# A hybrid conv and gated-DeltaNet block: first products of three projections tile by tile, and a last norm in halves

## Chip, cores and metric

One core of one Trainium2 chip. The metric is device time in microseconds of one execution of the whole block; lower is better.

## The reference

The block is two half-step SwiGLU feed-forward layers around a mixer, with norms in fp32, for 1024 tokens of 1024 channels:

```python
h = h + 0.5 * swiglu_ffn(rmsnorm(h, ffn1_norm), ffn1_w_in, ffn1_w_out)
u = rmsnorm(h, mix_norm) @ w_mix_in
...
h = h + jnp.concatenate([y_conv, y_gdn], axis=-1) @ w_mix_out
h = h + 0.5 * swiglu_ffn(rmsnorm(h, ffn2_norm), ffn2_w_in, ffn2_w_out)
return rmsnorm(h, final_norm)
```

The hidden width of the feed-forward layers is 2816. The mixer is a short gated convolution beside a chunked gated delta rule of four heads.

## The kernel before

**Products.** Activations lie with channels on the 128 partitions and half of the tokens (512) along the row: `h[hf][d]`, token half `hf`, channel tile `d` of eight. Every large product is one level of Strassen's method in Winograd's form: seven products of half size from blocks of the activations (A11, A12, S1, nS2, S3, S4, A22) and of the weights (B11 to B22, T1 to T4, the T being differences of B). Each fp32 factor is split in two parts, high and low: `split` casts on ScalarE (L102) and subtracts on VectorE (L103). `mm3` multiplies high by high, low by high, high by low (L191 to L193), three matmuls of 128x128 by 512 tokens that add into one PSUM bank. T sums are made on POOL (`pool_tt`, L110) in a ring of four buffers; weights arrive by SP's DMA queue in a ring of eight raw tiles; their parts, whi and wlo, are in a ring of seven.

**Order of the work.** `task(run, prep, load)` appends to a list; `run_tasks` goes through it, calling a task's prep 4 and its load 9 places ahead of its run. `mm3` calls `tick`, and `later(n, f)` calls f after n more of these; a norm uses it: `after(n, m)` calls `reduce` (sums of squares, L225) after n and `spread` (factors to all partitions, L243) m later. Each engine has its own queue in the order that results.

**First two pairs.** `all_pairs` runs the seven products for pairs of output tiles; it is called three times, for the first FFN's input (about 50 to 100 us), for the mixer's (700 to 760) and for the second FFN's (1295 to 1350). Each starts while the second half's norm is still to come. Once the factors `rb` are there, `Blocks.sums(0)` makes S1 and nS2 from the second half (L300, L301, four tiles each) and splits them; `sums(1)` makes A22, S3 and S4; `sums(2)` splits A22 and S4. `Pair.body` yields p6 (T2 x nS2), p5 (T1 x S1), p7 (T3 x S3), p4 (T4 x A22) and p3 (B22 x S4), each of 12 matmuls and each with its T made just ahead. p7 ends in the sum c on VectorE (L389, L390) into which the bank is read.

**The output products.** `ffn_out` runs seven products of 11 steps of 12 matmuls into two sets of four banks. The last two, S3 x T3 and A22 x T4, end in `add`: VectorE adds half of each bank into the residual (L554), and ScalarE and VectorE make the sum of squares for the next norm. `t1_done` and `out_t1` start the norm of the first half after the fifth product. At the end of the program `scale_out` scales the residual by the last norm's factors and weight on VectorE (L1387) and POOL (L1385) and stores it in eight DMAs of 256 KB per half (L1389).

Of the kernel before, what the change touches and what calls it, by code (L numbers as in the profile page):

```python
# [12 lines left out]
P = 128  # L13
D = 1024
# [42 lines left out]
def tile_hybrid(  # L57
# [209 lines left out]
    class Blocks:  # L267
# [53 lines left out]
    class Pair:  # L321
# [41 lines left out]

        def body(self):
# [44 lines left out]
    def all_pairs(pairs, x, norm2, between={}):  # L409


        norm2.then(lambda: x.sums(0, norm2.rb))
        for a in (0, 2):
            for n, two in enumerate(zip(*(p.body() for p in pairs[a:a + 2]))):
                if a == 0 and n in (1, 2):
                    task(None, lambda n=n: norm2.then(lambda: x.sums(n, norm2.rb)))
                for t in two:
                    task(*t)
# [77 lines left out]
    def ffn_out(acc, fill, g_dr, w_out, t1_done, t2_done):  # L496
# [8 lines left out]
        def step(banks, a, b, k, start):  # L505
# [27 lines left out]
            def run():  # L533
                x, w = ops["x"], ops["w"]
                if start and k == 0:
                    banks[:] = [psum() for _ in range(KH)]
                for d in range(KH):
                    ds = slice(d * P, (d + 1) * P)
                    mm3(banks[d], w[0][:, ds], w[1][:, ds], x[0], x[1], start and k == 0, k == NK - 1)

            task(run, ready, loads)

        def product(banks, a, b, start, *to, then=None, after=None):
            for k in range(NK):
                step(banks, a, b, k, start)
# [4 lines left out]
            def add():  # L550
                for d in range(KH):
# [9 lines left out]
            task(add)  # L561
# [8 lines left out]
        product(ba, "A22", "T4", True, "C21", then=t2_done)  # L570
# [19 lines left out]
    with ExitStack() as stack:  # L590
# [74 lines left out]
        def t1_done():  # L665
# [3 lines left out]
            nm[0].after(26, 4)  # L669
# [703 lines left out]
    with ExitStack() as stack:  # L1373
# [4 lines left out]
        def scale_out(hf):  # L1378
            rb = temp(F32, "rbs")
            nc.scalar.copy(out=rb, in_=last[hf].rb)  # L1380
            for d in range(KT):
                a = acc[hf][d]
                if d % 3 == 1:
                    nc.scalar.activation(out=a, in_=a, func=AF.Copy, scale=vcol(V_N["final"] + d))
                    nc.gpsimd.tensor_tensor(out=a, in0=a, in1=rb, op=ALU.mult)  # L1385
                else:
                    nc.vector.scalar_tensor_tensor(out=a, in0=a, scalar=vcol(V_N["final"] + d), in1=last[hf].rb,  # L1387
                                                   op0=ALU.mult, op1=ALU.mult)
                (nc.scalar if hf and d % 2 else nc.sync).dma_start(out=out[hf, d], in_=a)  # L1389
# [7 lines left out]
        ffn_out(acc, fill, g_dr, w2_out, out_t1, lambda d: last[1].square(d, nc.vector))  # L1397
        run_tasks()
        last[1].reduce()
        last[1].spread()  # L1400
        scale_out(1)
# [67 lines left out]
```

## Time and profile before

| | |
|---|---|
| median of 3 runs | 1960.46 us (1956.25 to 1960.53) |
| profiled execution | 1959.77 us, span 1958.0 us |
| busy: TensorE | 1833.8 us, 94% |
| VectorE, ScalarE, POOL | 68%, 38%, 37% |
| mean granted clock of TensorE | 0.971 |
| DMA | 312.45 MB, 160 GB/s over the span |

Busy time counts a matmul until its modelled end, so a TensorE that is busy all the time is not by that at its peak. The granted clock is 1.00 at the higher of its two levels and 0.50 at the lower.

### The profile page before, as it was taken

The numbers are of one execution on the slowest core, as the hardware profiler recorded it, in microseconds if no ns is written. First come the engines' busy times: TensorE is split into PE (matmuls) and PEld (weight loads), VectorE is DVE, ScalarE is ACT, GpSimd is POOL, SyncE is SP. The second block draws the span as 40 slices with busy tenths as digits, with TensorE's granted clock in tenths as the row PEclk, the third lists the DMA queues.
The fourth block names the chain that finished last, engine by engine and source line by source line (L and its number), as shares of the span: only waits on it lengthen the run. The fifth ranks groups of instructions, "written<-read, shape, count | busy, mean of one in ns | idle before, by whom it ended". The sixth has DMA issues, their size and how long they took to land.

```text
span 1958.0 us, 25016 instructions
## 1 busy us (share of the span) xinstructions
PE 1833.8 (94%) x8512; PEld 1493.6 (76%) x8512; DVE 1338.5 (68%) x1991; ACT 750.0 (38%) x1517; POOL 733.3 (37%) x510
## 2 busy tenths in 40 slices
PE   5799999999999899987799989998999999999996
PEld 4578888888888777676678877776888888888884
DVE  4876666567865797776974356688666566677655
ACT  6422323223544453377332243452323222344433
POOL 1464455355331434145311001036454355435142
PEclk9899999999999999998999979998999999999998
DMA  7144343437883423477742176423343434487532
GB/s 281 33 161 128 118 140 127 140 108 257 311 270 113 140 97 102 141 245 252 222 135 80 61 263 183 164 92 102 127 139 127 140 109 160 150 292 274 193 108 97
DMA packets 194512, 312.45 MB, mean 160 GB/s; under 512 B 27856, under 2 KB 48336, under 8 KB 194384
## 3 DMA queue, kind: packets, MB, share of 16 engines
q1 hardware_dynamic: 191216, 305.28, 47.0%
q10 hardware_dynamic: 3168, 5.57, 0.9%
q8 instruction: 67, 1.10, 0.2%
q14 instruction: 61, 0.50, 0.1%
HBM read 228.44 MB, written 82.33 MB: 159 GB/s over the span
## 4 chain that ended last, share of the span: by engine, by line
PE 74%; DVE 13%; issue 4%; DMA 3%; POOL 3%; ACT 3%; SPq 0%; POOLq 0%; DVEq 0%; ACTq 0%
PE ps_ps L192 20%; PE ps_ps L191 20%; PE ps_ps L193 20%; PE ps_mm L191 3%; PE ps_mm L192 3%; PE ps_mm L193 3%; DVE wlo L103 3%; PE ps_aux L862 1%; DVE lo L103 1%; DVE xb L1034 1%; DVE sv L1030 1%; DVE cv L774 1%; POOL T L110 1%; DMA raw<-w_in 1%; DVE h L301 1%
## 5 line engine op out<-in xcount | busy, mean ns | idle before, releaser
L191 PE MATMUL ps_ps<-hi,whi 128*128 128x512 f32 x1400 | 554.1, 396 | 23.0 <-DVE c L389 11.4
L193 PE MATMUL ps_ps<-hi,wlo 128*128 128x512 f32 x1400 | 552.7, 395 | 13.0 <-DVE wlo L103 12.9
L192 PE MATMUL ps_ps<-lo,whi 128*128 128x512 f32 x1400 | 553.0, 395 | 5.3 <-DVE lo L103 5.2
L103 DVE TENSOR_TENSOR wlo<-raw,whi 128x512 fp32r<-128x512 f32 x280 | 267.3, 964 | 119.4 <-ACT whi L102 118.4
L103 DVE TENSOR_TENSOR wlo<-T,whi 128x512 fp32r<-128x512 f32 x244 | 235.3, 978 | 144.5 <-ACT whi L102 142.4
L191 PEld LDWEIGHTS ps_ps<-hi,whi 128*128 128x128 f32 x1400 | 266.8, 191 | 85.4 <-issue 12.3
L193 PEld LDWEIGHTS ps_ps<-hi,wlo 128*128 128x128 f32 x1400 | 267.3, 191 | 71.7 <-DVE wlo L103 16.0
L192 PEld LDWEIGHTS ps_ps<-lo,whi 128*128 128x128 f32 x1400 | 266.9, 191 | 63.1 <-DVE lo L103 8.0
L110 POOL TENSOR_TENSOR T<-raw 128x512 f32<-128x512 f32 x144 | 224.6, 1561 | 232.3 <-DMA raw<-w_out 91.5
L191 PE MATMUL ps_ps<-ghi,whi 128*128 128x512 f32 x616 | 241.8, 393 | 7.2 <-ACT whi L102 7.2
L192 PE MATMUL ps_ps<-glo,whi 128*128 128x512 f32 x616 | 241.9, 393 | 1.4 <-DVE glo L103 1.4
L193 PE MATMUL ps_ps<-ghi,wlo 128*128 128x512 f32 x616 | 241.7, 393 | 1.2 <-DVE wlo L103 1.2
L102 ACT CAST whi<-raw 128x512 fp32r<-128x512 f32 x280 | 170.2, 617 | 86.1 <-PE ps_mm L192 19.1
L102 ACT CAST whi<-T 128x512 fp32r<-128x512 f32 x244 | 146.4, 617 | 81.4 <-POOL T L110 44.8
L191 PE MATMUL ps_mm<-hi,whi 128*128 128x512 f32 x384 | 158.0, 412 | 0.9 <-DVE u L400 0.9
L192 PE MATMUL ps_mm<-lo,whi 128*128 128x512 f32 x384 | 155.2, 404 | 1.2 <-DVE lo L103 1.2
L193 PE MATMUL ps_mm<-hi,wlo 128*128 128x512 f32 x384 | 154.2, 402 | 1.4 <-DVE wlo L103 1.4
L103 DVE TENSOR_TENSOR glo<-raw,ghi 128x512 fp32r<-128x512 f32 x154 | 128.9, 838 | 38.8 <-ACT ghi L102 37.2
L191 PEld LDWEIGHTS ps_ps<-ghi,whi 128*128 128x128 f32 x616 | 116.3, 189 | 33.6 <-ACT whi L102 8.4
L193 PEld LDWEIGHTS ps_ps<-ghi,wlo 128*128 128x128 f32 x616 | 116.3, 189 | 28.0 <-DVE wlo L103 2.7
L192 PEld LDWEIGHTS ps_ps<-glo,whi 128*128 128x128 f32 x616 | 116.4, 189 | 27.3 <-DVE glo L103 2.1
L110 POOL TENSOR_TENSOR T<-raw,T 128x512 f32<-128x512 f32 x50 | 73.3, 1465 | 167.2 <-DMA raw<-w_in 129.3
(226 smaller groups left out, 2286.5 us busy)
## 6 DMA issues: line engine op xcount, KB each, us to landing
raw<-w_in SPq DMA_DIRECT2D x264, 256.0 KB, 4.6
raw<-w_out SPq DMA_DIRECT2D x154, 256.0 KB, 4.3
raw<-w_qkv SPq DMA_DIRECT2D x36, 256.0 KB, 3.4
f1S<-S SPq DMA_DIRECT2D x33, 256.0 KB, 5.0
raw<-f1A SPq DMA_DIRECT2D x33, 256.0 KB, 3.9
raw<-f1S SPq DMA_DIRECT2D x33, 256.0 KB, 3.7
f2S<-S SPq DMA_DIRECT2D x33, 256.0 KB, 5.0
raw<-f2A SPq DMA_DIRECT2D x33, 256.0 KB, 4.5
```

The source lines that it names most:

```text
L102: tc.keep_in_program_order(nc.scalar.copy(out=hi, in_=src))
L103: nc.vector.tensor_tensor(out=lo, in0=src, in1=hi.bitcast(F32), op=ALU.subtract)
L110: tc.keep_in_program_order(nc.gpsimd.tensor_tensor(out=out, in0=in0, in1=in1, op=op))
L191: nc.tensor.matmul(out=ps, lhsT=whi, rhs=xhi, start=start, stop=False, skip_group_check=True)
L192: nc.tensor.matmul(out=ps, lhsT=whi, rhs=xlo, start=False, stop=False, skip_group_check=True)
L193: nc.tensor.matmul(out=ps, lhsT=wlo, rhs=xhi, start=False, stop=stop, skip_group_check=True)
L301: nc.vector.tensor_tensor(out=s2, in0=s2, in1=s1, op=ALU.subtract)
L774: nc.vector.scalar_tensor_tensor(out=acc, in0=u[:, i:i + HALF], scalar=vcol(wc + i), in1=acc, op0=ALU.mult, op1=ALU.add)
L862: nc.tensor.matmul(out=ps[:, sl], lhsT=lhs[:, sl], rhs=rhs[:, sl], start=start, stop=stop)
L1030: nc.vector.tensor_tensor(out=tv, in0=lrow[:, lo:hi].unsqueeze(2).broadcast_to([nb, n, j + 1]), in1=xrow[:, 0:j + 1].unsqueeze(1).broadcas ...
L1034: nc.vector.tensor_tensor(out=xv, in0=xv, in1=tv, op=ALU.subtract)
```

## The change

Four places change. (1) In `all_pairs` the products T1 x S1 and T2 x nS2 of the first two pairs run tile by tile: for each k, both products of both pairs, in four banks; S1's split follows directly on its scaling. The preps of T1 and T2 come first for both pairs, and A22's and S4's splits come behind T3's prep. (2) Two norms are started earlier: `after(26, 4)` and `after(30, 4)` become `after(14, 4)`. (3) In the second FFN's last product the last four steps are held and run bank by bank, each bank's `add` right behind it. (4) The last norm and its scaling run in two halves of 256 tokens, with 16 stores of 128 KB, ten on SP's queue and six on ScalarE's; the final weight is applied ahead for three of eight channel tiles (`gain`).

```diff
                     nc.vector.tensor_tensor(out=s2, in0=s2, in1=s1, op=ALU.subtract)
+                    b["S1"][k] = split(s1, slot)
                     b["nS2"][k] = split(s2, slot)
-                for k in range(KH):
-                    b["S1"][k] = split(h[1][k], slot)
...
+        def both(self, k):
+            if k == 0:
+                self.z, self.y = psum(), psum()
+            ks = slice(k * P, (k + 1) * P)
+            for ps, t, s in ((self.z, "T1", "S1"), (self.y, "T2", "nS2")):
+                w = self.w[t]
+                mm3(ps, w[0][:, ks], w[1][:, ks], *self.x.b[s][k], k == 0, k == KH - 1)
+            if k == KH - 1:
...
+                nc.vector.tensor_tensor(out=self.u2[:, 3:HALF + 3], in0=self.y, in1=self.p1[:, 3:HALF + 3], op=ALU.add)
...
+            products = list(zip(*(p.body() for p in pairs[a:a + 2])))
+            if a == 0:
+                for one, two in zip(*products[:2]):
+                    task(None, one[1], one[2])
+                    task(None, two[1])
+                for k in range(KH):
+                    task(lambda k=k: [p.both(k) for p in pairs[:2]])
+            for n, two in enumerate(products):
+                if a == 0 and n == 1:
+                    task(None, lambda: norm2.then(lambda: x.sums(1, norm2.rb)))
+                if a > 0 or n > 1:
+                    for t in two:
+                        task(*t)
+                if a == 0 and n == 2:
+                    task(None, lambda: norm2.then(lambda: x.sums(2, norm2.rb)))
...
-        product(ba, "A22", "T4", True, "C21", then=t2_done)
+        product(ba, "A22", "T4", True, "C21", then=t2_done, by_tile=by_tile)
...
+            for d in range(KH):
+                task(lambda d=d: [one(d, i == KH - 1) for i, one in enumerate(held)] and add([d]))
...
-            nm[0].after(26, 4)
+            nm[0].after(14, 4)
...
-            last[0].after(30, 4)
-            last[0].then(lambda: scale_out(0))
+            last[0].after(14, 4)
+            last[0].then(lambda: [gain(0, d) for d in range(KT) if pre_scaled(d)] and scale_out(0))
...
+        ffn_out(acc, fill, g_dr, w2_out, out_t1, out_t2, by_tile=True)
         run_tasks()
-        last[1].reduce()
-        last[1].spread()
-        scale_out(1)
...
+        for i in range(2):
+            for b in range(2 * i, 2 * i + 2):
+                nc.tensor.matmul(out=last[1].rb[:, b * P:(b + 1) * P], lhsT=rs[:, b:b + 1].broadcast_to([P, P]),
+                                 rhs=ident, start=True, stop=True)
+            scale_out(1, slice(2 * i * P, (2 * i + 2) * P))
```

How the order moves, in three places. First VectorE's queue in the first FFN's first products, before. Here h_81 to h_84 are S1's tiles, h_73 to h_76 those of nS2 and then of S3, h_85 to h_88 those of A22; T1_522 and T1_544 (before) are the two pairs' T1.

```order
L103 TENSOR_TENSOR lo_610<-h_74,hi_609 128x512
L313 TENSOR_TENSOR h_76<-h_76,h_88 128x512
L103 TENSOR_TENSOR lo_618<-h_75,hi_617 128x512
L103 TENSOR_TENSOR wlo_646<-T1_522,whi_645 128x512
L103 TENSOR_TENSOR lo_626<-h_76,hi_625 128x512
L103 TENSOR_TENSOR wlo_666<-T1_544,whi_665 128x512
L380 TENSOR_TENSOR u2_682<-ps_ps_669,p1_439 128x512
L103 TENSOR_TENSOR lo_685<-h_85,hi_684 128x512
L380 TENSOR_TENSOR u2_729<-ps_ps_716,p1_441 128x512
```

The same place in the changed kernel, where T1_593 and T2_595 belong to the second pair:

```order
L103 TENSOR_TENSOR lo_586<-h_84,hi_585 128x512
L307 SCALAR_TENSOR_TENSOR h_85<-h_85,vs_66,ps_ps_548 128x512
L103 TENSOR_TENSOR lo_590<-h_76,hi_589 128x512
L103 TENSOR_TENSOR wlo_598<-T2_595,whi_597 128x512
L103 TENSOR_TENSOR wlo_616<-T1_593,whi_615 128x512
L312 TENSOR_TENSOR h_73<-h_73,h_85 128x512
L307 SCALAR_TENSOR_TENSOR h_86<-h_86,vs_66,ps_ps_548 128x512
L307 SCALAR_TENSOR_TENSOR h_87<-h_87,vs_66,ps_ps_548 128x512
```

T1's last low part stood behind three of S3's subtractions; now it stands ahead of all of S3's, right behind S1's and nS2's. A little further on the same queue, before, where s4 is S4:

```order
L103 TENSOR_TENSOR lo_689<-h_86,hi_688 128x512
L103 TENSOR_TENSOR lo_693<-h_87,hi_692 128x512
L103 TENSOR_TENSOR lo_697<-h_88,hi_696 128x512
L103 TENSOR_TENSOR lo_701<-s4_598,hi_700 128x512
L103 TENSOR_TENSOR lo_705<-s4_606,hi_704 128x512
L103 TENSOR_TENSOR lo_709<-s4_614,hi_708 128x512
L103 TENSOR_TENSOR lo_713<-s4_622,hi_712 128x512
L103 TENSOR_TENSOR wlo_734<-T3_731,whi_733 128x512
L103 TENSOR_TENSOR wlo_746<-T3_743,whi_745 128x512
```

And in the changed kernel:

```order
L103 TENSOR_TENSOR lo_666<-h_76,hi_665 128x512
L103 TENSOR_TENSOR wlo_688<-T3_685,whi_687 128x512
L103 TENSOR_TENSOR wlo_706<-T3_703,whi_705 128x512
L103 TENSOR_TENSOR lo_728<-h_85,hi_727 128x512
L374 TENSOR_TENSOR u2_773<-ps_ps_678,p1_441 128x512
L103 TENSOR_TENSOR lo_732<-h_86,hi_731 128x512
L103 TENSOR_TENSOR lo_736<-h_87,hi_735 128x512
L103 TENSOR_TENSOR lo_740<-h_88,hi_739 128x512
```

T3's low parts stood behind the eight subtractions for A22 and S4; now they stand ahead of them. On TensorE's queue the twelve matmuls of T2 x nS2, which took nS2's tiles one after the other for one pair, and those of T1 x S1 behind them, are now mixed: three matmuls with a tile of S1 into one bank, three with the tile of nS2 into another, then the same for the second pair. Third, TensorE's queue at the end of the program, before:

```order
L193 MATMUL ps_ps<-ghi,wlo 128x512
L225 MATMUL ps_ps<-cs,nacc 128x1 [waits DVE_49]
L225 MATMUL ps_ps<-cs,nacc 128x1 x3
L243 MATMUL ps_ps<-cs,rs 128x128 [waits Pool_49]
L243 MATMUL ps_ps<-cs,rs 128x128 x3
```

and now, where L1453 is the reduction and L1460 the spread:

```order
L193 MATMUL ps_ps<-ghi,wlo 128x512
L1453 MATMUL ps_ps<-cs,nacc 128x1 [waits DVE_49]
L1453 MATMUL ps_ps<-cs,nacc 128x1
L1453 MATMUL ps_ps<-cs,nacc 128x1 [waits DVE_49]
L1453 MATMUL ps_ps<-cs,nacc 128x1
L1460 MATMUL ps_ps<-cs,last_rs 128x128 [waits Pool_49]
L1460 MATMUL ps_ps<-cs,last_rs 128x128
L1460 MATMUL ps_ps<-cs,last_rs 128x128 [waits DVE_49,Pool_49]
L1460 MATMUL ps_ps<-cs,last_rs 128x128
```

The reduction and the spread are in two parts, and the second part of each has a wait of its own for VectorE. In the same way the norm's spread at the end of the first FFN stands 36 matmuls earlier on TensorE's queue, and that at the end of the second FFN 48 earlier.

## Rows read from the trace of the kernel before

**Rows 1.** The page: the chain that ended last, shares of the span by engine.

```profile
PE 74%; DVE 13%; issue 4%; DMA 3%; POOL 3%; ACT 3%; SPq 0%; POOLq 0%; DVEq 0%; ACTq 0%
```

**Rows 2.** Windows, 100 to 640 us: each engine's busy us (x instructions), granted clock, DMA share, GB/s.

```profile
100.00:640.00 540.00, 538.38 (x2367) 443.79 (x2366) 364.82 (x430) 181.74 (x324) 244.57 (x161) 1.00 0.50 169
```

**Rows 3.** Waits of PE, 50 to 100 us: for what, us in total, times, longest.

```profile
PE ps_ps L193 <- DVE wlo L103: 7.3, 2, 6.2
PE ps_ps L191 <- DVE c L389: 2.9, 1, 2.9
```

**Rows 4.** Timeline of DVE at 57.9 us: start, length, line, operation, out<-in.

```profile
57.92 1.77 DVE L301 TENSOR_TENSOR h<-h 128x512 f32<-128x512 f32 x1
```

**Rows 5.** Timeline of POOL at 71 us; in brackets its idle time before and what ended it.

```profile
71.34 2.20 POOL L110 TENSOR_TENSOR T<-raw 128x512 f32<-128x512 f32 x1 [9.90 <-DVE wlo L103]
```

**Rows 6.** Windows: five stretches right after waits of PE, with their matmuls and granted clock.

```profile
71.25:75.25 4.00, 4.00 (x10) 3.21 (x11) 4.00 (x6) 3.13 (x6) 3.89 (x2) 0.51 0.14 34
88.80:92.00 3.20, 3.20 (x9) 2.53 (x8) 2.32 (x4) 0.00 (x0) 1.07 (x1) 0.50 0.02 5
733.75:737.25 3.50, 3.50 (x9) 2.73 (x10) 1.68 (x2) 1.05 (x2) 3.40 (x3) 0.53 0.15 44
1328.98:1334.98 6.00, 6.00 (x15) 4.70 (x16) 4.05 (x4) 2.28 (x4) 5.82 (x4) 0.52 0.29 90
1918.30:1921.80 3.50, 3.46 (x8) 2.57 (x9) 3.50 (x5) 3.50 (x7) 1.70 (x2) 0.51 0.47 137
```

**Rows 7.** Waits of PE, 700 to 760 us (mixer's projection).

```profile
PE ps_ps L193 <- DVE wlo L103: 3.0, 2, 2.2
PE ps_ps L191 <- DVE c L389: 2.5, 1, 2.5
PE ps_ps L191 <- ACT whi L102: 1.1, 1, 1.1
```

**Rows 8.** Waits of PE, 1295 to 1350 us (second FFN's first products).

```profile
PE ps_ps L191 <- DVE c L389: 3.2, 1, 3.2
PE ps_ps L193 <- DVE wlo L103: 2.6, 2, 2.2
PE ps_ps L191 <- ACT whi L102: 1.2, 1, 1.2
```

**Rows 9.** Waits of PE, 640 to 680 us (end of the first FFN).

```profile
PE ps_ps L191 <- ACT whi L102: 3.1, 2, 2.2
PE ps_ps L193 <- DVE wlo L103: 1.2, 2, 0.8
PE ps_ps L192 <- DVE glo L103: 0.7, 1, 0.7
```

**Rows 10.** Windows: VectorE's load at 60, 632 and 660 us.

```profile
60.00:70.00 10.00, 4.65 (x18) 3.23 (x18) 10.00 (x17) 6.19 (x12) 1.45 (x1) 0.92 0.00 0
632.00:642.00 10.00, 10.00 (x54) 8.54 (x53) 0.76 (x3) 0.00 (x0) 3.84 (x4) 1.00 0.21 56
660.00:670.00 10.00, 7.83 (x34) 5.81 (x32) 6.93 (x8) 5.28 (x10) 9.65 (x7) 1.00 0.46 157
```

**Rows 11.** Waits of PE, 1880 us to the end.

```profile
PE ps_ps L191 <- ACT whi L102: 4.1, 1, 4.1
PE ps_ps L225 <- DVE nacc L211: 3.5, 1, 3.5
```

**Rows 12.** Timeline of all engines, 1942 us to the end.

```profile
1942.83 1.87 PE L225 MATMUL ps_ps<-cs,nacc 128*128 128x1 f32 x8 [3.49 <-DVE nacc L211]
...
1948.78 3.38 DVE L1387 SCALAR_TENSOR_TENSOR h<-h,vs,ps_ps 128x512 f32<-128x512 f32 x5 [3.88 <-ACT rbs L1380]
...
1950.12 3.98 ACTq L1389 DMA_DIRECT2D out_dram<-h  x4
```

**Rows 13.** DMA issues: out<-in, queue, issues, KB each, median us from issue to landing.

```profile
raw<-w_out SPq DMA_DIRECT2D x154, 256.0 KB, 4.3
...
y_dr<-zt SPq DMA_DIRECT2D x16, 128.0 KB, 2.2
```

More of the change, by code (lines that the diff above doesn't have):

```diff
@@ L493, in early_heads, with ffn_out @@
             task(*p.head2())
[L496 removed]
+    def ffn_out(acc, fill, g_dr, w_out, t1_done, t2_done, by_tile=False):
         tsum = {}
@@ L503, in get, with step @@
             return load(w_out[2 * k + row][:, c * HALF:(c + 1) * HALF])
-        def step(banks, a, b, k, start):
+        def step(banks, a, b, k, start, held=None):
             r, ops = {}, {}
@@ L537, in run, with one, product @@
                 for d in range(KH):
[L538 to L543, printed above, removed]
+                    one(d, k == NK - 1)
+            def one(d, stop):
+                x, w = ops["x"], ops["w"]
+                ds = slice(d * P, (d + 1) * P)
+                mm3(banks[d], w[0][:, ds], w[1][:, ds], x[0], x[1], start and k == 0, stop)
+            if held is None:
+                task(run, ready, loads)
+            else:
+                held.append(one)
+                task(None, ready, loads)
+        def product(banks, a, b, start, *to, then=None, after=None, by_tile=False):
+            held = []
             for k in range(NK):
-                step(banks, a, b, k, start)
+                step(banks, a, b, k, start, held if by_tile and k >= NK - KH else None)
                 if KH <= k < KT:
@@ L548, in product, with add @@
                         task(lambda tile_=tile_: fill(*tile_))
-            def add():
-                for d in range(KH):
+            def add(ds=range(KH)):
+                for d in ds:
                     for n in to:
@@ L559, in add @@
                     after()
-            task(add)
+            if not by_tile:
+                task(add)
+                return
+            for d in range(KH):
+                task(lambda d=d: [one(d, i == KH - 1) for i, one in enumerate(held)] and add([d]))
         ba, bb = [], []
@@ L1393, in out_t1, with out_t2 @@
                 last[0].square(d)
-            last[0].after(30, 4)
-            last[0].then(lambda: scale_out(0))
-        ffn_out(acc, fill, g_dr, w2_out, out_t1, lambda d: last[1].square(d, nc.vector))
-        run_tasks()
-        last[1].reduce()
-        last[1].spread()
-        scale_out(1)
+            last[0].after(14, 4)
+            last[0].then(lambda: [gain(0, d) for d in range(KT) if pre_scaled(d)] and scale_out(0))
+        def out_t2(d):
+            last[1].square(d, nc.vector)
+            if pre_scaled(d):
+                gain(1, d)
+        ffn_out(acc, fill, g_dr, w2_out, out_t1, out_t2, by_tile=True)
+        run_tasks()
+        last[1].rb = psum()
+        sums = psum()
+        ms, rs = (const.tile([P, 4], F32, name=n) for n in ("last_ms", "last_rs"))
+        for i in range(2):
+            two = slice(2 * i, 2 * i + 2)
+            for b in range(2 * i, 2 * i + 2):
+                nc.tensor.matmul(out=sums[:, b:b + 1], lhsT=last[1].acc[:, b * P:(b + 1) * P], rhs=ones[:, 0:1],
+                                 start=True, stop=True)
+            nc.vector.tensor_scalar(out=ms[:, two], in0=sums[:, two], scalar1=1.0 / D, scalar2=EPS,
+                                    op0=ALU.mult, op1=ALU.add)
+            nc.gpsimd.tensor_tensor(out=rs[:, two], in0=ms[:, two], in1=pneg[:, two], op=ALU.pow)
+        for i in range(2):
+            for b in range(2 * i, 2 * i + 2):
+                nc.tensor.matmul(out=last[1].rb[:, b * P:(b + 1) * P], lhsT=rs[:, b:b + 1].broadcast_to([P, P]),
+                                 rhs=ident, start=True, stop=True)
+            scale_out(1, slice(2 * i * P, (2 * i + 2) * P))
         while queue:
```

30 lines of the change are left out of this document (15 added, 15 removed).

## The prediction

> **What bounds the kernel now.** I read the chain of waits first: TensorE holds 74% of the chain that ended last and VectorE 13% [rows 1], so time is to be had only where TensorE stands still. The windows by stage come next. In the longest undisturbed stretch TensorE is busy 538.38 of 540 us with 2367 matmuls at a granted clock of 1.00 [rows 2], which is 0.2275 us per matmul; whatever an earlier stage saves therefore passes through to the end. Then I read the waits of TensorE in the five stretches that the change touches, the stretches behind those waits in which the clock is at the lower of its two levels [rows 6], and the timeline of the last 20 us. A matmul at the lower level takes 4.0/10 = 0.40 us in the first of those stretches, so a stretch costs its length less 0.2275 us for each matmul in it.
>
> The sum is made against the profiled execution, 1959.77 us (span 1958.0); the median of the runs shown, 1960.46, is 0.7 above it. A measurement of this kernel can tell about 0.3% (5.9 us) from no change.
>
> **Part 1: first two pairs of the three input projections (first FFN, mixer, second FFN).** Nothing is computed less. Moved: VectorE's subtractions (lo parts), POOL's T3 and T4, ScalarE's casts, and the matmuls of T1·S1 and T2·nS2, which now run k by k.
>
> First FFN. TensorE waits 7.3 us for wlo parts (6.2 for T1's, 1.1 for T3's) and 2.9 for the c sum [rows 3]; two slow stretches follow, 4.0 - 10 x 0.2275 = 1.7 and 3.2 - 9 x 0.2275 = 1.2 [rows 6]. What is late is T1's low part: its subtraction stands behind those of nS2, S1 and three of S3. T3 needs a buffer that this subtraction reads last, and POOL sat 9.90 us until it had, T3 starting at 71.34 [rows 5]. In the new order T1's last subtraction stands eleven places earlier on VectorE (69 to 58), and T3's two stand before those of A22 and S4. So 7.3 + 2.9 + 2.9 = 13.1 us can go. What comes: a tile k of both pairs is 12 matmuls, 2.7 us, and VectorE must deliver four operations for it, 4 x 0.68 = 2.7 us by the duration of one (3.38/5 [rows 12]), but up to 1.77 each where POOL works beside it [rows 4]; I allow 1.7 us of small waits. T3's cast and subtraction still come behind the S3 parts: 3.0 us. T4: 0.7. A slow stretch after T3's wait: 2.0, between the two seen. Gain 13.1 - 7.4 = **5.7**, bounds 1 (only the c wait and little else goes) and 11.
>
> Mixer. Goes: 3.0 + 2.5 + 1.1 = 6.6 of waits [rows 7] and 1.5 of slow clock (3.5 - 9 x 0.2275) [rows 6] with 1.2 for the stretch after the c wait, taken from the like one in the first FFN. Comes: a weight of the second head, whose subtraction now stands three lo parts later, 1.0, and 0.7 at T4. Gain 9.3 - 1.7 = **7.6**, bounds 3 and 9.3.
>
> Second FFN. Goes: 3.2 + 2.6 + 1.2 = 7.0 [rows 8], slow clock 6.0 - 15 x 0.2275 = 2.6 [rows 6] and 1.2 as before, 10.8. Comes: the second head's weight stands behind 15 VectorE operations in place of 12 here, and POOL's T and s4 sums run beside them. Three at 0.68 are 2.0 us, at 1.77 they are 5.3; I take 2.5, since TensorE wanted it only just before it was ready. A slow stretch behind that wait 2.0, T4 0.5. Gain 10.8 - 5.0 = **5.8**, bounds 1 and 10.
>
> **Part 2: norm of the first half, end of the first FFN** (call count 26 to 14: 12 triples of matmuls, 36 x 0.2275 = 8.2 us sooner). The eight scalings and eight subtractions behind that norm now land where VectorE is busy 0.76 of 10 us [rows 10], in front of the casts of the last product. They cost about the 16 x 0.68 = 11 us that they took before, covered by that idle time. TensorE's waits behind it, 3.1 for whi, 1.2 for wlo and 0.7 for glo [rows 9], should go: 5.0, of which I leave 0.5. **4.5**, bounds 2 and 5.5. The sum of squares is done before the earlier call, so the reduce waits for nothing; if POOL's adds were late, TensorE's queue would hold there for a few POOL operations.
>
> **Part 3: norm at the end of the second FFN and the last product** (30 to 14: 48 matmuls, 10.9 us sooner). POOL's scaling of the first half came between the T4 sums before; TensorE waited 4.1 us for whi [rows 11] and then ran a slow stretch, 3.5 - 8 x 0.2275 = 1.7 [rows 6]. With the norm ahead of the final product's preparations the casts are done in time. Gain 5.8 - 0.3 = **5.5**, bounds 3 and 6.5. The 44 triples run bank by bank only in their last four steps; all of those casts must be there before the first of four banks ends, and VectorE's queue should reach the last of them about 2 us before it is wanted (an estimate, from some 14 operations of 0.68 us behind the adds).
>
> **Part 4: the end.** Now all four banks' adds come behind the last matmul; TensorE waits 3.5 us for the sum of squares [rows 11]. In the new order only bank 3's add, square and sum remain, three operations of about 0.68, so 3.5 - 2.0 = 1.5 is saved. Behind it stand the reduction at 1942.83, VectorE's five scalings from 1948.78 (3.38 us), and the output's issues, the last from 1950.12 on; the span ends at 1958.0 [rows 12]. Two halves overlap the scaling of one with the output of the other. The final bytes are 1 MB in place of 2 MB; the first half leaves about 2 us sooner. TensorE's second reduction waits for VectorE's reading of the first bank, and the second spread for VectorE's reading of the first half's, so the halves are only partly abreast. Added are a second copy of the factors, five more operations on VectorE and three on POOL, each of half the length, and eight more output issues; they lie beside each other or beside the first half's output. I take 2.5 here: **4.0** in all, bounds 1 and 5.5. Sixteen output transfers of 128 KB take the place of eight of 256 KB; the only 128 KB stores in the trace land in 2.2 us against 4.3 for a load of 256 KB [rows 13], so I charge nothing for the size.
>
> A rule speaks against this. The Trainium skill, page "DMA: Bandwidth & Descriptors", section "Rules for kernel authors", wants 1 MiB or more in one transfer for the highest bandwidth, by which pieces of 128 KB would be the wrong way. By that rule part 4 would gain only the 1.5 of the adds; the rows on 128 KB do not agree, and it is rival (d).
>
> Sum: 5.7 + 7.6 + 5.8 + 4.5 + 5.5 + 4.0 = 33.1. From 1959.8: **1927 us**.
>
> **Rivals.** (a) *The waits move.* VectorE is full in this stretch (10.00 of 10 us in 60 to 70 us [rows 10]) and the change takes no operation off it; so the three sites stay as long as they are and only parts 2 to 4 pay, 14.0: 1946 us. For it: the full engine. Against: the waits are on single late operations, and those are moved ahead. 13%.
> (b) *Slower: the tile order keeps TensorE below its clock.* Working tile by tile over four banks TensorE stops for each lo part; should the clock go to its lower level through those 48 matmuls at each site, each costs 0.40 - 0.2275 = 0.17 more, 8.3 us a site, 25 in three; with the waits of part 1 as they are, and parts 2 to 4 gained, 1959.8 - 14.0 + 25 = 1971 us. It decides from the granted clock at 57 to 70 us, 724 and 1300. For it: 10 matmuls at 0.51 right behind a wait of 6.2. Against: 660 to 670 us lost 2.2 of 10 us in waits and stayed at 1.00 [rows 10]. 3%. The Trainium skill, page "TensorE: Matmul & The Clock Gate", section "A second HAM failure mode: psum-queue depth-cycling", describes this: a kernel that cycled through banks and paused between groups swung between the two clock levels. By that rule 1971 would come; the trace, cycling four banks at 1.00 for 540 us, does not agree.
> (c) *The held steps of the last product come late.* Four steps' casts must all be there at one time, and a load of raw data takes 4.3 us to land [rows 13]. If the first bank's fourth step waits for one, 4.3 us of part 3 are lost: 1931 us. 8%.
> (d) *The output in small pieces is no quicker,* each issue paying its fixed time twice as often: the 2.5 of part 4 is lost, 1930 us. 4%.
> (e) *Nearly every moved wait vanishes,* with all bounds at their upper ends: 11 + 9.3 + 10 + 5.5 + 6.5 + 5.5 = 47.8, 1912 us. For it: the waits have few causes. 8%.
> (f) *No measurable change,* because a gain in one product is waited for in the next: 4%. Something unforeseen and slower: 2%.
>
> **How the numbers follow.** My forecast has 58%. Faster by over 0.3%: 58 + 13 + 8 + 4 + 8 = 91 of 100; within 0.3%: 4 of 100; slower: 3 for (b) and 2 for the rest. The range reaches from (e), 1912, to (a), 1946, and leaves out (b), (f), the unforeseen and about half of (a) and (e), which may end beyond these times: 2 in 10.
>
> **What would show it.** Right: no 6.2 us wait for T1's wlo; POOL's first T3 near 65 us; granted clock 1.00 from 60 to 70; no waits for c behind the raw weights; no 4.1 us wait at the second FFN's end; from the last matmul (1942.83 - 3.49 = 1939.3 [rows 12]) to the end near 15 us in place of 18.7. Wrong: a new wait of 2 us or more for the second head's weight, a clock below 1.00 in the tile-wise products, or the last bank waiting for casts.

## The result, and the profile after

The changed kernel took 1930.65 us (median of 4 runs, 1928.61 to 1931.09) against 1958.36 us of the kernel before (4 runs on the same chip): a ratio of 0.9857, with a 95% interval of 0.9834 to 0.9879, so 24 to 33 us faster. The forecast was 1927 us, in a range of 1912 to 1946. The profiled execution has a span of 1926.9 us, 31.1 less than the one before. The medians are 27.7 us apart here and 22.9 in experiment 10; the parts below sum to 23.4. That the time falls so close to the forecast is partly luck, as the section after the experiments shows. Two executions in the experiments, of 3988.5 us (2) and 3956.9 us (11), took twice as long as the others of their kernel and are left out of the medians.

The chain that ended last has become more of TensorE (74% in [rows 1]):

```profile
PE 76%; DVE 12%; DMA 3%; issue 3%; ACT 3%; POOL 2%; SPq 0%; POOLq 0%; DVEq 0%; ACTq 0%
```

The waits of TensorE in the first FFN's first products (what for, us in total, times, longest), to be held against [rows 3]:

```profile
PE ps_ps L191 <- DVE c L401: 2.4, 1, 2.4
PE ps_ps L191 <- DVE u L374: 2.2, 1, 2.2
PE ps_ps L193 <- DVE wlo L103: 1.7, 3, 1.1
PE ps_ps L192 <- DVE lo L103: 1.0, 2, 0.7
PE ps_ps L191 <- DVE c L402: 0.5, 1, 0.5
```

The 6.2 us for T1's low part are gone. In their place stand 2.2 us that the profile puts down to the u sum (L374; it reads T2 x nS2 out of the bank in which T3 x S3 goes on), and the c sum still costs 2.4 + 0.5. The cast of T3's weight, which T3 x S3 needs as well, ends at the same moment as u, near 73.05 us; TensorE goes on at 73.22:

```profile
72.39 0.68 DVE L374 TENSOR_TENSOR u<-ps_ps,p 128x512 f32<-128x512 f32 x1
72.43 1.14 ACT L102 CAST whi<-T 128x512 fp32r<-128x512 f32 x2
```

The windows (each engine's busy us, granted clock) show the clock that rival (b) turns on, beside the first of [rows 10]:

```profile
60.00:70.00 10.00, 7.80 (x31) 5.16 (x30) 10.00 (x14) 3.47 (x6) 5.52 (x4) 1.00 0.16 51
70.00:80.00 10.00, 7.42 (x25) 5.33 (x24) 10.00 (x14) 7.06 (x15) 5.57 (x3) 0.83 0.15 43
80.00:90.00 10.00, 6.98 (x23) 4.59 (x22) 10.00 (x13) 2.22 (x5) 4.91 (x4) 0.83 0.11 39
```

The tile-wise products run from 56.4 to 71.0 us, most of them in the first of these stretches, and the clock is at 1.00 there, where it was 0.92; it falls to 0.83 in the two stretches behind, after the waits for u and c. At the other two places, where the tile-wise products run from 709.8 and from 1301.8 us on without a wait, it is 1.00 too:

```profile
708.00:722.00 14.00, 12.87 (x57) 10.27 (x55) 12.16 (x18) 8.19 (x17) 11.33 (x6) 1.00 0.20 58
1300.00:1310.00 10.00, 10.00 (x46) 8.29 (x45) 9.59 (x15) 7.47 (x15) 3.91 (x2) 1.00 0.09 32
```

POOL's first T3 starts 7.9 us earlier than in [rows 5]:

```profile
63.40 1.73 POOL L110 TENSOR_TENSOR T<-raw 128x512 f32<-128x512 f32 x1
```

In the mixer's projection the three waits of [rows 7] have become one long one:

```profile
PE ps_ps L191 <- DVE u L374: 6.0, 1, 6.0
PE ps_ps L193 <- DVE wlo L103: 1.2, 1, 1.2
```

In the second FFN's projection the waits for the c sum, T3 and its cast of [rows 8] are down to 1.5, and the second head's weight, which the forecast had at 2.5 us, costs 3.2:

```profile
PE ps_ps L193 <- DVE wlo L103: 3.2, 1, 3.2
PE ps_ps L191 <- DVE c L401: 1.5, 2, 1.1
```

At the end of the first FFN, against 5.0 us in [rows 9]:

```profile
PE ps_ps L193 <- DVE wlo L103: 0.7, 2, 0.4
```

At the end of the second FFN no wait for casts is left (4.1 in [rows 11]); what remains is the end of the program:

```profile
PE ps_ps L1460 <- POOL h L1427: 2.6, 1, 2.6
PE ps_ps L1453 <- DVE nacc L211: 2.2, 1, 2.2
```

The timeline of the end, against [rows 12] (L1453 reduction, L1460 spread, L1429 VectorE's scaling):

```profile
1912.95 0.61 PE L1453 MATMUL ps_ps<-cs,nacc 128*128 128x1 f32 x4 [2.17 <-DVE nacc L211]
...
1916.27 2.05 DVE L1429 SCALAR_TENSOR_TENSOR h<-h,vs,ps_ps 128x256 f32<-128x256 f32 x5 [1.66 <-ACT rbs L1423]
...
1918.47 1.19 PE L1460 MATMUL ps_ps<-cs,last_rs 128*128 128x128 f32 x4 [2.64 <-POOL h L1427]
...
1920.10 2.05 DVE L1429 SCALAR_TENSOR_TENSOR h<-h,vs,ps_ps 128x256 f32<-128x256 f32 x5 [1.78 <-ACT rbs L1423]
```

The last matmul ends at 1912.95 - 2.17 = 1910.78, so 16.1 us before the end; before it was 18.7.

### The profile page after: what moved, and what is told of

It reads as the page before. It is cut to its first block, busy times and chain, and to the rows that moved or that the text cites. A ratio compares the mean times of both kernels' runs of the same rounds, so it can differ in the third digit from the quotient of the medians.

```text
span 1926.9 us, 25042 instructions
## 1 busy us (share of the span) xinstructions
PE 1821.5 (95%) x8512; PEld 1484.2 (77%) x8512; DVE 1336.7 (69%) x1997; ACT 751.7 (39%) x1518; POOL 741.2 (38%) x514
## 4 chain that ended last, share of the span: by engine, by line
PE 76%; DVE 12%; DMA 3%; issue 3%; ACT 3%; POOL 2%; SPq 0%; POOLq 0%; DVEq 0%; ACTq 0%
PE ps_ps L193 21%; PE ps_ps L191 21%; PE ps_ps L192 21%; PE ps_mm L191 2%; PE ps_mm L192 2%; DVE wlo L103 2%; PE ps_mm L193 2%; DVE lo L103 2%; PE ps_aux L898 1%; DVE xb L1070 1%; DVE sv L1066 1%; DVE cv L810 1%; POOL nrm L1030 1%; DMA raw<-w_in 1%; PE ps_aux L940 1%
## 5 line engine op out<-in xcount | busy, mean ns | idle before, releaser
L103 DVE TENSOR_TENSOR wlo<-raw,whi 128x512 fp32r<-128x512 f32 x280 | 261.7, 943 | 115.2 <-ACT whi L102 110.4
L103 DVE TENSOR_TENSOR wlo<-T,whi 128x512 fp32r<-128x512 f32 x244 | 231.1, 961 | 142.8 <-ACT whi L102 142.4
L110 POOL TENSOR_TENSOR T<-raw,T 128x512 f32<-128x512 f32 x50 | 77.0, 1540 | 157.9 <-DMA raw<-w_in 113.8
```

The lines of the kernel that those rows point to most:

```text
L103: nc.vector.tensor_tensor(out=lo, in0=src, in1=hi.bitcast(F32), op=ALU.subtract)
L110: tc.keep_in_program_order(nc.gpsimd.tensor_tensor(out=out, in0=in0, in1=in1, op=op))
```

## Where the time went, stretch by stretch

In both traces TensorE's rows can be counted from the start, and the time between the starts of the same two matmuls compared. That shows each place by itself, free of what came ahead of it. All 8512 matmuls are in every trace, and the borders lie in undisturbed stretches. (The expectations below name the long unedited stretch by a count in which some matmuls are missing: 513.8 us there is 508.4 here, 508.8 is 504.4.) The table is worked out in this way from all profiles of this study: the old order is the kernel before and one or two variants that go back to it in this place, the changed order the changed kernel, its second profile and the variants with that place unaltered.

| stretch (matmul from, to) | old order, us | changed order, us (mean, range) | gain | forecast |
|---|---|---|---|---|
| first FFN's start (0, 450) | 133.8, 132.3 | 131.1 (129.6 to 132.7), 7 profiles | 1.9 | 5.7 |
| end of first FFN (2550, 2850) | 72.8, 72.8 | 67.5 (67.1 to 67.7), 12 | 5.3 | 4.5 |
| mixer's projection (2850, 3150) | 78.2, 78.2 | 77.1 (76.1 to 77.6), 7 | 1.1 | 7.6 |
| second FFN's projection (5700, 6150) | 115.0, 113.8 | 108.7 (107.7 to 110.4), 7 | 5.7 | 5.8 |
| end of second FFN (8150, 8450) | 74.0, 74.3 | 67.4 (67.0 to 69.1), 10 | 6.7 | 5.5 |
| last matmul to the end | 18.7 | 16.0 (15.2 to 16.6), 7 | 2.7 | 4.0 |

The sum of the gains is 23.4 us; the forecast's was 33.1. In the first row the scatter lies mostly ahead of the edited products and behind them: between matmuls 112 and 230 alone it is 43.5 us in both profiles of the old order and 40.7 (40.5 to 41.2) in the seven of the changed one, a gain of 2.8. The stretch of the mixer between the rows (matmuls 3150 to 5700), in which no line was edited, took 508.4 us before and 504.4 in the first profile of the change. That difference, 4.0 us, is about half of what the first pair of profiles shows beyond the sum (31.1 - 23.4 = 7.7).

## The experiments

Each is the changed kernel with the edit shown; times are medians. The kernel before ran beside them on each chip: 1956.65 us beside 1 to 4, 1958.67 beside 5 to 8, 1957.87 beside 9 to 12. The changed kernel itself gave 1930.65 and 1934.99 us (experiment 10), so a difference of some 4 us between medians of different chips says nothing; the stretches repeat better.

**1. The pairs' order undone** (`u_pairs`): `sums(0)` splits S1 after nS2, and `all_pairs` goes product by product as before.

```diff
-                    b["S1"][k] = split(s1, slot)
+                for k in range(KH):
+                    b["S1"][k] = split(h[1][k], slot)
...
+            for n, two in enumerate(zip(*(p.body() for p in pairs[a:a + 2]))):
+                if a == 0 and n in (1, 2):
+                    task(None, lambda n=n: norm2.then(lambda: x.sums(n, norm2.rb)))
+                for t in two:
+                    task(*t)
```

> The first two pairs of the three projections go back to the order of before, the norms and the end stay changed. Theory A (what the two traces show place by place, by the start of the same matmul in both): 4.1 us in the first FFN, 1.8 in the mixer, 5.5 to 7 in the second FFN, so 11 to 13 us of the gain are given back: about 1942 to 1944 us. Theory B (the forecast's sizes, 5.7 + 7.6 + 5.8 = 19.1, with something else in the mixer hiding a part): about 1950 us. Theory C (the 3 us that the mixer's later part gained come from this part too): about 1946 us. The 6.0 us wait for the u sum in the mixer's projection should be gone, and the waits of 2.2 and 2.5 us there for wlo and c back.

Measured: 1938.88 us (ratio to before 0.9913, interval 0.9890 to 0.9936), 8.2 above the changed kernel's median; below what each theory gave. It is 17.8 us below the kernel before on its chip, where the changed kernel was 27.7 and 22.9 below on others, so the runs alone say 5 to 10 us. The stretches say 7.4: 132.3, 78.2 and 113.8 us against the table's 131.1, 77.1 and 108.7. The mixer's waits are those of before again, in the same three places, and yet the stretch takes only 1 us more than in the changed order:

```profile
PE ps_ps L193 <- DVE wlo L103: 3.1, 2, 2.3
PE ps_ps L191 <- DVE c L402: 2.7, 1, 2.7
PE ps_ps L191 <- ACT whi L102: 1.2, 1, 1.2
```

So in the mixer the change had put one wait of 6.0 us in the place of waits that sum to 7.0.

**2. Both first-half norms late again** (`u_norms`).

```diff
-            nm[0].after(14, 4)
+            nm[0].after(26, 4)
...
-            last[0].after(14, 4)
+            last[0].after(30, 4)
```

> Both first-half norms go back to their later calls (26 and 30), all else stays changed. Theory A: the 5.2 us at the end of the first FFN and the 6.7 at the end of the second come from the earlier calls: about 1942 us. Theory B: at the second FFN's end the bank-by-bank last product gives TensorE other work while it would wait, so that only the 5.2 come back: about 1936 us.

Measured: 1948.57 us (0.9964, interval 0.9944 to 0.9983; 9 runs). The two stretches come back in full: 72.8 us at the end of the first FFN (67.5 changed) and 74.3 at the end of the second (67.1), 12.5 us together. Theory A on the mechanism: bank by bank takes no part in the second gain, since it was kept here. The median is 7 us above what A gave; no stretch that was edited accounts for these 7.

**3. The end as before** (`u_end`): steps in the last product, norm and output in one piece.

```diff
-        ffn_out(acc, fill, g_dr, w2_out, out_t1, out_t2, by_tile=True)
+        ffn_out(acc, fill, g_dr, w2_out, out_t1, out_t2, by_tile=False)
...
+        last[1].reduce()
+        last[1].spread()
+        scale_out(1)
```

> The last product by steps again, the last norm and its output in one piece, all else stays changed. Theory A: the 3.1 us that the traces show between the last product and the end come back: about 1933.8 us. Theory B: the held steps cost TensorE something in the last product that the traces hide, so less than 2 us come back: 1932 us or below.

Measured: 1937.34 us, with runs from 1930.8 to 1944.0 (0.9901, interval 0.9868 to 0.9934). From the last matmul to the end it took 17.6 us in place of 16.0: 1.6 come back, half of what A gave; the median lies above both theories. Of the 1.1 us to the 18.7 of before, 0.5 lies in the eight matmuls of the reduction (1.87 us before, 1.40 here) and 0.6 between the start of VectorE's scaling and the end (9.3 and 8.7). There this variant keeps the changed division of the stores, five on SP's queue and three on ScalarE's in place of four and four; that this is the cause is not shown.

**4. VectorE's order mended** (`u2_first`): the subtractions for A22 and S4 are kept behind what was written ahead of them on VectorE, and `sums(2)` is written one task later, behind the u sums.

```diff
+        ins = nc.vector.tensor_tensor(out=lo, in0=src, in1=hi.bitcast(F32), op=ALU.subtract)
+        if pin:
+            tc.keep_in_program_order(ins)
...
-                    b["A22"][k] = split(h[1][k + KH], slot)
+                    b["A22"][k] = split(h[1][k + KH], slot, pin=True)
...
+                    task()
                     task(None, lambda: norm2.then(lambda: x.sums(2, norm2.rb)))
```

> VectorE's subtractions for A22 and S4 are pinned behind the u sums that free the bank in which T3 x S3 goes on. Theory A (in the mixer TensorE waits 6.0 us, in the first FFN 2.2, because four to five of these subtractions stand ahead of the u sums, up to 1.43 us each beside POOL): both waits go, with some 1.5 us of lower clock behind each, and A22's low parts come up to 1 us late: 6 to 9 us faster, 1922 to 1925 us. Theory B (VectorE is full there, so that any order makes TensorE wait as long, for A22's parts or the c sum in place of the u sum): 1929 to 1932 us, with a new wait of 4 us or more ahead of T4 x A22.

What it mends is this piece of VectorE's timeline in the changed kernel (start, length, line): T3's low part, then four subtractions for A22, one for S4, and only then the u sum that frees the bank.

```profile
718.72 1.15 DVE L103 TENSOR_TENSOR wlo<-T,whi 128x512 fp32r<-128x512 f32 x1 [1.83 <-ACT whi L102]
719.79 5.73 DVE L103 TENSOR_TENSOR lo<-h,hi 128x512 fp32r<-128x512 f32 x4
725.45 0.68 DVE L103 TENSOR_TENSOR lo<-s,hi 128x512 fp32r<-128x512 f32 x1
726.05 0.68 DVE L374 TENSOR_TENSOR u<-ps_ps,p 128x512 f32<-128x512 f32 x1
```

The four take 5.73 us, 1.43 each. In the variant the u sums come first:

```profile
721.09 1.17 DVE L103 TENSOR_TENSOR wlo<-T,whi 128x512 fp32r<-128x512 f32 x1 [1.84 <-ACT whi L102]
722.17 0.68 DVE L376 TENSOR_TENSOR u<-ps_ps,p 128x512 f32<-128x512 f32 x1
723.30 0.69 DVE L376 TENSOR_TENSOR u<-ps_ps,p 128x512 f32<-128x512 f32 x1 [0.45 <-PE ps_ps L195]
723.91 4.21 DVE L103 TENSOR_TENSOR lo<-h,hi 128x512 fp32r<-128x512 f32 x4
```

Measured: 1928.13 us (0.9846, interval 0.9821 to 0.9871). The wait for u is gone from the mixer's projection, and so are the waits for the c sum but for 0.5:

```profile
PE ps_ps L195 <- DVE wlo L103: 1.6, 2, 1.2
PE ps_ps L193 <- DVE c L403: 0.5, 1, 0.5
```

That stretch now takes 70.1 us, 7.0 below the changed order's mean and 8.1 below the old order. Theory A in the mixer; the variant pins the subtractions and also writes them one task later, and the two are not told apart. In the first FFN the wait stays at 2.2: there the first u sum does not stand behind A22's subtractions but behind S3's, which the variant does not move, and T3's cast ends together with it. The total is 3 us short of A.

**5. A bank of its own for T3 x S3** (`own_bank`).

```diff
+                if self.own:
+                    self.y = psum()
+                prod(self.y, self.w.pop("T3"), self.x.b["S3"], self.own)
...
+                nc.vector.tensor_tensor(out=inner(c), in0=self.y, in1=inner(self.u2 if self.own else self.p1), op=ALU.add)
```

> T3 x S3 of the first two pairs goes into a bank of its own, so that it need not wait for the u sum; VectorE's order is that of the changed kernel, and c and the fourth product's sum add u in place of p. Theory A (the wait for the u sum is a matter of the bank alone): no wait for u in the first FFN (2.2 us) and the mixer (6.0); from the last matmul of the tile-wise products to the same place in the mixer (78.2 us before, 76.4 changed, 70.2 with the pinned order, for 300 matmuls) about 71; total 1922 to 1926 us. Theory B (VectorE's queue, not the bank: four subtractions of A22 beside POOL also stand ahead of the c sum and of S4's parts): the wait moves to the c sum, 74 to 77 us for that stretch, total 1928 to 1932 us.

Measured: 1931.77 us (0.9858, interval 0.9833 to 0.9883). Theory B: the wait moved from the u sum to the c sum,

```profile
PE ps_ps L191 <- DVE c L405: 4.8, 1, 4.8
PE ps_ps L193 <- DVE wlo L103: 1.2, 1, 1.2
```

and the stretch took 76.0 us. On VectorE the order is that of the changed kernel: A22's four subtractions, then u, then c, one 10 us behind the start of the four.

```profile
722.13 5.78 DVE L103 TENSOR_TENSOR lo<-h,hi 128x512 fp32r<-128x512 f32 x4
...
728.44 0.68 DVE L376 TENSOR_TENSOR u<-ps_ps,p 128x512 f32<-128x512 f32 x1
...
732.65 0.67 DVE L405 TENSOR_TENSOR c<-ps_ps,u 128x512 f32<-128x512 f32 x1
```

So the bank alone was not the cause. The same four subtractions, and S4's behind them, held up whatever came next. In the first FFN the wait for u went as well, and T3's cast came into its place:

```profile
PE ps_ps L191 <- ACT whi L102: 2.1, 1, 2.1
```

**6. A22 ahead of T3 again** (`a22_first`), which undoes only the order of these casts.

```diff
+                if a == 0 and n == 2:
+                    task(None, lambda: norm2.then(lambda: x.sums(2, norm2.rb)))
                 if a > 0 or n > 1:
                     for t in two:
                         task(*t)
-                if a == 0 and n == 2:
-                    task(None, lambda: norm2.then(lambda: x.sums(2, norm2.rb)))
```

> A22's and S4's splits go ahead of T3's prep again, the tile-wise products and all else stay changed. Theory A (T3's casts ahead of A22's are worth what T3's low parts waited): TensorE waits for T3's low parts again, 2 to 4 us at each of the three projections, and the u sum's wait stays or grows, since the subtractions still stand ahead of it: 1934 to 1942 us. Theory B (the tile-wise products alone bring the gain, since VectorE has to do these subtractions before T4 in either order): within 3 us of the changed kernel, 1928 to 1933 us.

Measured: 1938.42 us (0.9888, interval 0.9860 to 0.9916). The total is A's, the places are not: in the first FFN TensorE waits 6.2 us ahead of T3 x S3 and the stretch takes 135.9 us against 131.1 (the waits, then a row of ScalarE),

```profile
PE ps_ps L191 <- DVE lo L103: 6.2, 1, 6.2
PE ps_ps L191 <- DVE c L401: 3.2, 1, 3.2
```

```profile
77.54 1.13 ACT L102 CAST whi<-T 128x512 fp32r<-128x512 f32 x2
```

The profile names VectorE's low parts, but the first of T3's two casts on ScalarE, which stand behind the eight of A22 and S4 now, ends near 78.1 us and TensorE goes on at 78.20; S3's last low part had been done at 74.6. In the mixer it is better than in the changed kernel, 74.1 us against 77.1, and in the second FFN the same, 108.6 against 108.7.

```profile
PE ps_ps L191 <- DVE c L401: 2.5, 1, 2.5
```

T3 ahead of A22 is worth some 5 us at the first of three places and costs 3 at the second. No single order is best in all three.

**7. Two banks for the last factors** (`rb_two`).

```diff
+            if i:
+                last[1].rb = psum()
```

> The second half of the last norm's factors goes into a bank of its own. Theory A (the second spread waited 2.6 us because VectorE still read the bank of the first half): the second spread follows the first without that wait, VectorE's ten scalings run one behind the other, and from the last matmul to the end 14 to 14.8 us in place of 16.1; about 1929 us in total, not to be told from 1930.7 by runs. Theory B (it waited for POOL, which the profile names as its releaser): the wait stays, 16 us.

Measured: 1935.77 us (0.9878, interval 0.9834 to 0.9922; 2 runs, with the unedited stretch of the mixer at 511.1 us in the profile). From the last matmul to the end 14.8 us in place of 16.0, and 14.8 and 15.3 in experiments 11 and 12, which keep this edit. Both spreads are one group of eight rows, and VectorE's ten scalings run without a gap:

```profile
1928.12 1.57 PE L1462 MATMUL ps_ps<-cs,last_rs 128*128 128x128 f32 x8 [0.18 <-POOL last_rs L1457]
...
1929.27 4.01 DVE L1429 SCALAR_TENSOR_TENSOR h<-h,vs,ps_ps 128x256 f32<-128x256 f32 x10 [1.14 <-ACT rbs L1423]
```

Theory A. The profile had named POOL as the releaser of the second spread; in the timeline of the changed kernel above, VectorE's five scalings end at 1916.27 + 2.05 = 1918.32 and the spread starts at 1918.47, and with the bank taken away the wait went while POOL's work stayed.

**8. One store per tile** (`out_whole`), with the halves kept.

```diff
-                (nc.scalar if hf and pre_scaled(d) else nc.sync).dma_start(out=out[hf, d][:, cut], in_=a)
+                if cut.stop == HALF:
+                    (nc.scalar if hf and pre_scaled(d) else nc.sync).dma_start(out=out[hf, d], in_=acc[hf][d])
```

> The last norm and its scaling stay in halves, but each tile of 256 KB is stored once, after its second half (as the first token half's are), in place of two stores of 128 KB. Theory A (early output of the first half is what the halves gain; small stores cost nothing): all 2 MB leave behind 1920.5, at about 340 GB/s 6 us and 2 to land, so from the last matmul to the end 17.5 to 18.5 us. Theory B (the rule that large transfers are faster: 128 KB stores lose what the early start gains): 16 us or less.

Measured: 1940.83 us (0.9904, interval 0.9866 to 0.9942; 2 runs), and 17.7 us from the last matmul to the end against 16.0. Theory A. The output's rows (KB each, median us to landing), first of the changed kernel, then of this variant:

```profile
out_dram<-h SPq DMA_DIRECT2D x10, 128.0 KB, 2.3
```

```profile
out_dram<-h SPq DMA_DIRECT2D x5, 256.0 KB, 3.7
```

and a microsecond in the middle of the last output of each (granted clock, DMA share and GB/s at the end of the row):

```profile
1923.00:1924.00 1.00, 0.00 (x0) 0.00 (x0) 0.00 (x0) 0.00 (x0) 0.00 (x0) 0.50 1.03 339
```

```profile
1929.00:1930.00 1.00, 0.00 (x0) 0.00 (x0) 0.00 (x0) 0.00 (x0) 0.00 (x0) 0.50 1.03 377
```

The small stores land 1.4 us sooner and run at 339 GB/s against 377. The size alone does not make the 3.7: in the kernel before, stores of the same 256 KB on SP's queue land in 2.2 us at this place,

```profile
out_dram<-h SPq DMA_DIRECT2D x4, 256.0 KB, 2.2
```

so what makes the 3.7 is open. What the run shows is the worth of the early start.

**9. The last product by steps, the halves kept** (`steps_end`).

```diff
-        ffn_out(acc, fill, g_dr, w2_out, out_t1, out_t2, by_tile=True)
+        ffn_out(acc, fill, g_dr, w2_out, out_t1, out_t2, by_tile=False)
```

> The last product goes by steps again, the last norm and its output stay in halves. Theory A (bank by bank saves the adds of three banks behind the last matmul): TensorE waits 3.5 us for the sum of squares in place of 2.2, and from the last matmul to the end 17.4 us in place of 16.1; the stretch before it is unchanged at 67.0 us. Theory B (held steps also relieve the casts in that stretch): it grows by 2 us or more.

Measured: 1937.88 us (0.9894, interval 0.9860 to 0.9928; 2 runs). Theory A: the stretch before is 67.0 us, unchanged, the wait for the sum of squares is 3.5 again, and the end takes 17.8 us.

```profile
PE ps_ps L1453 <- DVE nacc L211: 3.5, 1, 3.5
```

**10. The changed kernel again** (`after_again`), unedited, beside the next two on one chip.

> The changed kernel itself, beside the two combinations on the same chip: 1930.7 us again, within 3. The stretch of the mixer in which no instruction was edited (2550 matmuls behind its projection) took 513.8 us before and between 505.7 and 515.1 in the variants. Theory A (that is scatter of the execution): another value between 505 and 515. Theory B (the change reaches into it): 508.8 again within 0.5.

Measured: 1934.99 us (0.9888, interval 0.9863 to 0.9913), 22.9 below the 1957.87 of before on this chip. In its profile (span 1941.0) the unedited stretch of the mixer took 514.1 us where the first profile of the same program had 504.4; in the fourteen profiles of the study it lies between 503.5 and 514.1. Theory A, with more scatter than expected; the median is 4.3 us above the 1930.7 that was expected within 3.

**11. The mended order and the two banks together** (`best2`), the edits of 4 and 7.

> The pinned order of A22's and S4's subtractions together with the two banks at the end. Theory A (the two gains, 6.2 us in the mixer's projection and 1.4 at the end, are on TensorE's path and add up): 7.6 us below the changed kernel's median on this chip, about 1923 us. Theory B (the mixer's projection is waited for by the recurrence behind it, which takes the 6 us back): 2 us below, about 1928.5 us.

Measured: 1927.40 us (0.9851, interval 0.9823 to 0.9878), 7.6 below the changed kernel on the same chip. Theory A: the mixer's projection takes 70.1 us and the end 14.8. This version has a lower median than both kernels; against the changed one the runs overlap (1926.2 to 1936.5, 1929.8 to 1942.8), and the two stretches carry the claim.

**12. With the bank of its own as well** (`best3`), the edits of 4, 5 and 7.

> As the last, with T3 x S3 in a bank of its own as well. Theory A (with VectorE's order mended, the bank still costs the 2.2 us that TensorE waits for u in the first FFN, and nothing in the mixer): 2 us below the last, about 1921 us. Theory B (the wait goes to the c sum, as it did with the bank alone): the same as the last within 1 us.

Measured: 1927.53 us (0.9844, interval 0.9818 to 0.9870), the same as the last. Theory B: in the first FFN the u sum's 2.2 us went, a wait of 2.1 for T3's cast came, and the c sum's rose from 2.4 to 4.4.

## Why the prediction was right, and where it was not

**Direction and bounds.** It was right that TensorE's waits in five places are what the change can win, that they pass through, and that all five places and the end would gain. Each did, in the table; the time lies within the range. The sum was 40% too large: 33.1 for 23.4, and the mixer's 1.1 lies below the bound of 3 written for it.

**Part 1, mixer.** The step that failed: "Comes: a weight of the second head ... 1.0, and 0.7 at T4. Gain 9.3 - 1.7 = 7.6". What came is a wait of 6.0 us for the u sum, a stretch of lower clock behind it, and 1.2 for the head's weight; 1.1 was left of the gain. The clock in that stretch:

```profile
726.88:730.50 3.62, 3.62 (x9) 2.93 (x10) 3.45 (x6) 2.11 (x4) 0.69 (x1) 0.54 0.00 0
```

(3.62 - 9 x 0.2275 = 1.6 us.) The forecast had looked at T3's weight as the last thing that T3 x S3 waits for. With the weight early, the next late thing is the bank, and it is read by an operation that stands behind four subtractions moved there by this change. The mended order shows that the 7.6 were there to be had (8.1).

**Part 1, first FFN.** Forecast 5.7, measured 1.9 in the mean of seven profiles (4.2 in the first, 2.8 at the edited products alone). T1's wait of 6.2 went, as written, and T3's 1.1; the tile-wise products waited 0.7 for a low part, 1.1 for the second pair's weight and 0.4 in smaller waits, 2.2 for the 1.7 allowed. T3's 3.0 came as 2.2 + 0.4, and the cast of T3 alone would have made TensorE wait as long as u did (2.1 in experiment 5). The failed step is "So 7.3 + 2.9 + 2.9 = 13.1 us can go": the c sum's 2.9 did not go (2.4 + 0.5), nor did the two slow stretches, since the clock fell behind the waits for u and c as it had behind the old ones, to 0.83 in both windows above.

**Part 1, second FFN.** Forecast 5.8, measured 5.7: right. The head's weight costs 3.2 us for 2.5, and T3 and c nothing but 1.5. A wait of 2 us or more for that weight was one of the forecast's own signs of being wrong; it came, and the gain held, since the sum had charged for it.

**Parts 2 and 3.** Forecast 4.5 and 5.5, measured 5.3 and 6.7; both right in mechanism by experiment 2, and each about 1 us too small. In part 2 the waits fell from 5.0 to 0.7 us, 4.3; the rest is in what surrounds them. In part 3 no wait is left: 4.1 for whi, 0.6 for glo, which the forecast did not count, and the slow stretch of 1.7 went, 6.4. The held steps were in time, so rival (c) fell: the stretch takes 67.0 us with them and without them.

**Part 4.** Forecast 4.0, measured 2.7. The adds: TensorE's wait fell from 3.5 to 2.2, 1.3 where 1.5 was written; 1.8 of the end by experiment 9. The failed step is the term for the halves, "I take 2.5 here". With the last product by steps in both, one piece ends 14.1 us after the reduction's start (experiment 3) and halves 14.3 (experiment 9); over the eight profiles with unaltered halves it is 13.9 (13.0 to 14.4), and 15.2 before. So the halves brought between nothing and 1.3 us. The forecast knew that the second spread waits for VectorE's reading of the first half and had it "only partly abreast"; that wait is 2.6 us, and taking it away gives 1.1 (14.9 in the mean of three profiles for 16.0).

**Rivals.** (a) held for the mixer in the main and for the first FFN in part, where waits moved, and not for the second FFN. (b) fell: the granted clock is 1.00 in the tile-wise products at all three places, with waits of 0.1 to 1.1 us among them at the first. In the changed kernel's trace the falls of the clock in the three projections stand at waits of 2.2, 2.4, 6.0 and 3.2 us, none of them between tile-wise products. The swing between the two levels that the Trainium skill, page "TensorE: Matmul & The Clock Gate", section "A second HAM failure mode: psum-queue depth-cycling", describes was not seen here. (d) fell as a mechanism by experiment 8: with the halves kept, stores of 128 KB that start early beat stores of 256 KB by 1.7 us (16.0 and 17.7). Its price, the 2.5 of the halves, was lost in great part all the same. The rule of the Trainium skill, page "DMA: Bandwidth & Descriptors", section "Rules for kernel authors", that larger transfers give more bandwidth, agrees with the rate (339 against 377 GB/s there) and does not decide a transfer whose start is what is late.

**What the medians alone would have hidden.** The forecast stood 3.7 us from the median; by its parts it was off by 10. The first profile of the changed kernel had 4 us of scatter in its favour in a stretch that was not edited. So the time lies near the forecast by luck, and in the range by the mechanism.

## What to carry to other kernels

When an operand that comes late is moved ahead, ask what the consumer waits for next, and list each of its needs, the output bank too, with its place on the engine that releases it: here a wait of 6 us came from four subtractions that were made early and wanted late. Pin such operations behind the reader that frees a bank; where that reader's engine has a full queue, a second bank alone passed the wait on to the next reader (experiment 5), and at the end of the program, where the queue was empty, it took the wait away (experiment 7). Judge a change of many places by stretches of the trace between the same instructions, over several profiles, and not by the total, when an unedited stretch scatters by 10 us.

## What the hardware showed that was not expected

VectorE's subtractions with two operands in SBUF took 1.43 us each beside POOL's work in the mixer, against 2.48/4 = 0.62 us for A22's in the first FFN of `a22_first`, where POOL stood still (from 68.9 to 80.7 us):

```profile
75.10 2.48 DVE L103 TENSOR_TENSOR lo<-h,hi 128x512 fp32r<-128x512 f32 x4
```

And in the mixer one of POOL's sums took 6.43 us (its row is rough), against 1.5 each for the two behind it; it is 6.43 and 6.42 in `u2_first` and `own_bank` too:

```profile
711.60 6.43 POOL L110 TENSOR_TENSOR T<-raw 128x512 f32<-128x512 f32 x1 [2.59 <-DVE wlo L103]
...
718.03 3.00 POOL L110 TENSOR_TENSOR T<-raw,T 128x512 f32<-128x512 f32 x2
```

While that one ran, VectorE's subtractions beside it took 0.63 us each (three in 1.88 us from 714.40 on), so now the one engine's operations were long and now the other's. No run took POOL's work away from this place; the two engines are compared here, and the cause is not shown.

The unedited stretch of the mixer, a chain of short operations and transfers, took 504.4 and 514.1 us in two profiles of the same program. Why one execution is 10 us longer there than another was not settled.
